# Block sums of the up weights: formed by GpSimd in the front and loaded from DRAM, where they were formed in the up stage

## The chip, the core and the metric

The kernel runs on one core of a Trainium2 chip. A core has TensorE (matmuls, PE in the profile; its weight loads are PEld), VectorE (DVE), ScalarE (ACT), GpSimd (POOL) and SyncE (SP), which here only issues DMAs. All of them work on SBUF, 128 partitions wide; TensorE writes its results to PSUM. Each engine takes its instructions in a fixed order and waits on semaphores. The metric is the time of one execution on the device in microseconds, the median of some runs.

## The reference

One layer of a decoder trunk on 1024 tokens of width 1024, float32. The front mixes three branches and projects them; the second half is a gated feed-forward network, whose input product is the up stage:

```python
h = rms_norm(x, norm1[l]); z = h @ w_in[l]           # pool | q | k | v | u | v | 3 gates
merged = g[:, :, 0] * y_a + g[:, :, 1] * y_b + g[:, :, 2] * y_c
x = x + merged @ w_out[l]
h = rms_norm(x, norm2[l])
up = causal_dwconv(h @ w_up[l], conv_w[l], conv_b[l])   # w_up: 1024 x 5632
gate, val = jnp.split(up, 2, axis=-1)                   # 2816 columns each
x = x + (jax.nn.silu(gate) * val) @ w_down[l]
```

## The kernel before

**Products.** Every float32 factor is split into a high part (ScalarE, a copy rounded to fp32r, L86) and a low part (VectorE, the difference, L87); a product is three matmuls, high-high, high-low and low-high. A weight is loaded into one of three "raw" buffers, split into another buffer, and used.

**The front** goes over the tokens in two halves (t = 0, 1). Each half has the k/v, q and u/v products, then 26 units of 128 columns (`units`: two for pooling, 16 gates of the branches A and C, eight gates of branch B), each of 24 matmuls, after which a gated product of the unit before follows, and at the end the product with w_out. Attention, norms and rope are generators ("tasks") that `tick` advances when a planned clock, counted up with the matmuls that are written, reaches their time. The planned clock sets the order in which the program is written. A scheduler then orders each engine's stream by a timeline of its own, and a transfer whose buffer is free may be issued well ahead of its place in the text. `tc.issue_after(ins)` ties the order of instructions traced in its block to `ins`.

The half's input x is loaded again for the residual into the "x2" buffers (t = 0) or the "x" buffers (t = 1). `part` holds the sum of the branches A and C; it has one buffer. In the second half's w_out product `norm2_flip` normalizes and transposes the first half's result, which stands in x2[0] in SBUF.

**The up stage** uses a Strassen scheme (Winograd's form): for each of 22 chunks of 128 columns the gate block `g` (columns c) and the value block `v` (columns 2816 + c) of w_up are cut into an upper and a lower half of 512 rows, a11, a12 (gate) and a21, a22 (value). Four sums are formed of them by GpSimd (L858 to L861): s1 = a21 + a22, s2 = s1 - a11, s3 = a11 - a21, s4 = a12 - s2. Seven products P1 to P7 follow, each of four times three matmuls, one product being a turn. The first seven chunks do P1 and P2 early (PRE) and the rest later (REST); the other 15 do all in one go (FULL). `up_prep` prepares the weights of a chunk: its loads begin LOADS = 9 turns ahead, its splits are done READY = 7 turns ahead. VectorE adds the products up (L916, L919, L926, L928, L939) and does the convolution (L875) and the gate (L884) of the chunk before. Sums and several of the split weights stand in 13 "q" buffers.

**The down stage** does the same for w_down, from some 1080 us on, and is not touched.

Of the kernel before, what the change touches and what calls it, by code (L numbers as in the profile page):

```python
# [6 lines left out]
F32 = mybir.dt.float32  # L7
# [6 lines left out]
P = 128  # L14
# [19 lines left out]
N_PRE = 7  # L34
PRE_SETS = ((0, 1), (2, 3), (4, 5, 6))
LOADS, READY = 9, 7


def trunk_kernel(tc, x, positions, norm1, w_in, q_norm, k_norm, sinks, w_pool, pool_scale,
# [103 lines left out]
    clock = [0.0]  # L143
    tasks = []

    def tick():
        again = True
        while again:
            again = False
            for tk in list(tasks):  # L150
                if tk[0] <= clock[0] and tk in tasks:
                    step(tk)
                    again = True
# [14 lines left out]
            step(tk)  # L168


    def three(ps, a, b, first, last, n=T):

        pe.matmul(ps, a(0), b(0), start=first, stop=False)  # L173
        pe.matmul(ps, a(0), b(1), start=False, stop=False)  # L174
        r = pe.matmul(ps, a(1), b(0), start=False, stop=last)  # L175
        clock[0] += 3 * n * 0.216 / 512
        return r

# [423 lines left out]
    def up_split(src, wt):  # L602
        split(wt[:, 0], wt[:, 1], src)
        return wt

    def up_early(c):
        g = up_raw(0, c)
        return {n: up_split(a, slot("w", 4, [P, 2, HK, P], F32R)) for n, a in (("P1", g[:, 0:HK, :]), ("P2", g[:, HK:, :]))}
# [29 lines left out]
    x2, sss = [], []  # L638
    h2d = [dp.tile([P, 2, T], F32, name=f"h2d{k}") for k in range(4)]
    gd = [dp.tile([P, S], F32, name=f"gd{c}") for c in range(NC_FF)]  # L640
    mark = [None]
    spawn(setup_rest(), 24)
    st = Stream(w_in, 768, 256, KD, normed.ins)
    for t in range(2):
# [28 lines left out]
        mx = [slot("x", 4, [P, 2, T], F32R) for _ in range(2)]  # L673
        side = [spawn(sgu(u, v, sg))]
        tick()
        part = slot("part", 1, [P, KD, T], F32)
        mxs = [lambda q, m=m: m[:, q, :] for m in mx]
        sgs = [lambda q, m=m: m[:, q, :] for m in sg]
        qv = qa.rearrange("p b (e j q) -> p b e j q", e=2, j=4)
# [29 lines left out]

        wp = None  # L710
        for i, c0 in enumerate(units):
            if i + 1 < len(units):
                wn = w_gran(w_in, units[i + 1])
            else:
                x2t = [slot("x2" if t == 0 else "x", 4, [P, D], F32) for _ in range(NT)]
                for b in range(NT):
                    r = t * T + b * P
                    sp.dma_start(x2t[b], x[r : r + P, :])
                st = Stream(w_out, 0, T, KD)
            if i >= 2:  # L720
                kind, n = ((i - 2) % 2, (i - 2) // 2) if i < 18 else (2, i - 18)
                if kind != 1:
                    wp = proj_b(n) if kind == 2 else proj_ac(n)
            if i == 20 and t == 0:
                load_x(1)
                spawn(h_ahead(1, None))
            if i == 2:
                for q in qt:
                    need(q)
                for b in range(NT):  # L730
                    att.append(spawn(attention(t, b, qa, rqs), 4 + 24 * b))
            ps = mm_ps()
            chan_major(ps, wt, h)
            if i < 2:
                side.append(spawn(pooling(t, i, ps, mx)))
            else:
                th = slot("th", 3, [P, T], F32)
                act.activation(th, ps, AF.Tanh, scale=0.5)
                pend.append((kind, n, th, wp))
                if len(pend) > 1:  # L740
                    finish_unit()
            wt = wn
        while pend:
            finish_unit()
        while tasks:
            step(tasks[0])
        ss = slot("ssx", 2, [P, 32], F32)[:, 0:8]
        if t == 0:
            h = new_h()
            spawn(h_flip(1, h), 0.1)  # L750
        else:
            h2a = new_h()
            spawn(norm2_flip(x2[0], sss[0], h2a, 5, lambda: [a[:, q] for a in [at_ps()] for q in range(2)], 4))
# [82 lines left out]

    def up_prep(c, names):


        ws = wss[c, names]  # L840
        g = up_raw(0, c)
        if names == PRE:
            yield
            for n, a in (("P1", g[:, 0:HK, :]), ("P2", g[:, HK:, :])):
                ws[n] = up_split(a, slot("w", 4, [P, 2, HK, P], F32R))
                yield
            return
        v = up_raw(1, c)
        if names == REST:
            st = held.setdefault(c, {})  # L850
            st["s"], st["ug"] = sm2(), q_([P, S])
            sp.dma_start(st["s"], pre_d[c][:, 0, :])
            sp.dma_start(st["ug"][:, 0:T], pre_d[c][:, 1, :])
        a11, a12, a21, a22 = g[:, 0:HK, :], g[:, HK:, :], v[:, 0:HK, :], v[:, HK:, :]
        sa, sb = q_([P, 2, HK, P]), q_([P, 2, HK, P])
        s1, s2, s3, s4 = sa[:, 0], sa[:, 1], sb[:, 0], sb[:, 1]
        yield
        pool.tensor_tensor(s1, a21, a22, ALU.add)  # L858
        pool.tensor_tensor(s2, s1, a11, ALU.subtract)
        pool.tensor_tensor(s3, a11, a21, ALU.subtract)  # L860
        pool.tensor_tensor(s4, a12, s2, ALU.subtract)  # L861
        for n in names:
            wt = slot("w", 4, [P, 2, HK, P], F32R) if n in ("P1", "P6", "P2") else q_([P, 2, HK, P], F32R)
            ws[n] = up_split({"P1": a11, "P2": a12, "P3": s4, "P4": a22, "P5": s1, "P6": s2, "P7": s3}[n], wt)
            yield

    def conv(u, c):
# [324 lines left out]
```

## Time and profile before

| | |
|---|---|
| median of 3 runs | 1324.67 us (1323.91 to 1326.77) |
| profiled execution | 1327.64 us, its span 1325.9 us |
| TensorE busy | 1285.3 us, 97% of the span |
| VectorE busy | 974.4 us, 73% |
| ScalarE busy | 607.8 us, 46% |
| GpSimd busy | 189.5 us, 14% |
| read from and written to HBM | 120.3 MB and 29.9 MB |
| mean granted clock of TensorE | 0.994 of 2.4 GHz |

The span runs from the first to the last instruction; the execution's own time has some us around it. Busy time is what the profile counts as work of an engine; waiting for a semaphore and issuing a DMA on SP are not in it. Matmuls overlap, so the mean duration of one is longer than the distance from one to the next.

### The profile page before, as it was taken

How to read it: one execution, taken by the hardware profiler on the slowest of the kernel's cores; microseconds unless marked ns; L12 is line 12 of the kernel's file. 1: busy time of each engine (PE TensorE's matmuls, PEld its weight loads, DVE VectorE, ACT ScalarE, POOL GpSimd, SP SyncE). 2: the span in 40 equal slices, each digit the busy share in tenths (PEclk: the TensorE clock that was granted, in tenths of full speed). 3: DMA queues.
4: the chain of work that ended last, by engine and by line, in shares of the span. 5: the costliest groups of instructions: out<-in, count | busy, mean ns of one | idle time of the engine just before them, and what ended most of it. 6: DMA issues, size and time to landing. Idle time of an engine off the chain costs nothing.

```text
span 1325.9 us, 16088 instructions
## 1 busy us (share of the span) xinstructions
PE 1285.3 (97%) x5956; PEld 1064.1 (80%) x5956; DVE 974.4 (73%) x1520; ACT 607.8 (46%) x990; POOL 189.5 (14%) x123
## 2 busy tenths in 40 slices
PE   6999999999999999999999999999999998999996
PEld 6888888888888888888777878878778787788885
DVE  6887875644569776355585889889998885986986
ACT  5655554333465455333573444344444343444441
POOL 0000000000000000000005454245443400101202
PEclk9999999999999999999998999999999999999999
DMA  6422224422432222533554323333232256238705
GB/s 233 118 87 64 80 80 143 115 75 94 148 118 64 81 80 79 152 113 111 200 169 139 104 71 112 112 96 111 81 111 95 80 185 243 48 107 248 122 0 96
DMA packets 167644, 151.25 MB, mean 114 GB/s; under 512 B 7615, under 2 KB 132493, under 8 KB 167565
## 3 DMA queue, kind: packets, MB, share of 16 engines
q1 hardware_dynamic: 163533, 142.87, 33.9%
q0 software_dynamic: 4032, 7.34, 3.7%
q8 instruction: 47, 0.77, 0.2%
q14 instruction: 32, 0.26, 0.1%
HBM read 120.30 MB, written 29.88 MB: 113 GB/s over the span
## 4 chain that ended last, share of the span: by engine, by line
issue 53%; PE 19%; DVE 14%; DMA 5%; ACT 4%; POOL 0%; SPq 0%; POOLq 0%; DVEq 0%; ACTq 0%
DVE x L875 6%; PE bk L1129 4%; PE bk L1128 4%; PE bk L1130 4%; DVE q L87 3%; DMA raw<-in_w_up_dram 3%; PE bk L898 2%; PE bk L899 2%; PE bk L900 2%; ACT x L871 2%; DMA hq<-in_w_down_dram 1%; DVE w L87 1%; ACT w L86 1%; ACT x L883 1%; DVE x L87 1%
## 5 line engine op out<-in xcount | busy, mean ns | idle before, releaser
L175 PE MATMUL mm<-hh,w 128*128 128x512 f32 x416 | 162.6, 391 | 0.0
L173 PE MATMUL mm<-hh,w 128*128 128x512 f32 x416 | 162.6, 391 | 0.0
L174 PE MATMUL mm<-hh,w 128*128 128x512 f32 x416 | 162.4, 390 | 0.0
L87 DVE TENSOR_TENSOR w<-raw,w 128x1024 fp32r<-128x1024 f32 (+1 forms) x96 | 93.3, 976 | 89.5 <-ACT w L86 89.5
L858 POOL TENSOR_TENSOR q<-raw 128x512 f32<-128x512 f32 x22 | 35.6, 1617 | 847.4 <-DVE w L87 653.0
L86 ACT ACTIVATE w<-raw 128x1024 fp32r<-128x1024 f32 (+1 forms) x96 | 82.3, 858 | 155.8 <-PE mm L174 67.1
L875 DVE SCALAR_TENSOR_TENSOR x<-q,cA,x 128x1023 f32<-128x1023 f32 x88 | 136.2, 1554 | 22.8 <-ACT x L871 22.3
L898 PE MATMUL bk<-hq,q 128*128 128x512 f32 x352 | 139.2, 396 | 6.1 <-DVE sm L916 5.9
L899 PE MATMUL bk<-hq,q 128*128 128x512 f32 x352 | 138.0, 392 | 0.0
L900 PE MATMUL bk<-hq,q 128*128 128x512 f32 x352 | 137.6, 391 | 0.0
L1129 PE MATMUL bk<-x,w 128*128 128x512 f32 x308 | 121.1, 393 | 2.5 <-DVE x L87 2.5
L1130 PE MATMUL bk<-w,x 128*128 128x512 f32 x308 | 120.6, 392 | 0.0
L1128 PE MATMUL bk<-w 128*128 128x512 f32 x308 | 93.4, 391 | 4.1 <-ACT w L86 3.8
L174 PEld LDWEIGHTS mm<-hh,w 128*128 128x128 f32 x416 | 78.1, 188 | 16.1
L175 PEld LDWEIGHTS mm<-hh,w 128*128 128x128 f32 x416 | 78.1, 188 | 16.1
L173 PEld LDWEIGHTS mm<-hh,w 128*128 128x128 f32 x416 | 78.1, 188 | 15.7
L87 DVE TENSOR_TENSOR wa<-raw,wa 128x512 fp32r<-128x512 f32 x72 | 49.5, 695 | 55.5 <-ACT wa L86 55.5
L898 PEld LDWEIGHTS bk<-hq,q 128*128 128x128 f32 x352 | 66.6, 189 | 24.4 <-DVE sm L916 8.5
L871 ACT ACTIVATE x<-q,cA 128x1024 f32<-128x1024 f32 x44 | 54.0, 1241 | 68.7 <-DVE q L926 38.0
L86 ACT ACTIVATE wa<-raw 128x512 fp32r<-128x512 f32 x72 | 45.2, 631 | 79.5 <-PE mm L175 67.2
L900 PEld LDWEIGHTS bk<-hq,q 128*128 128x128 f32 x352 | 66.7, 189 | 14.0
L899 PEld LDWEIGHTS bk<-hq,q 128*128 128x128 f32 x352 | 66.7, 189 | 13.7
(267 smaller groups left out, 2957.6 us busy)
## 6 DMA issues: line engine op xcount, KB each, us to landing
raw<-in_w_in_dram SPq DMA_DIRECT2D x72, 512.0 KB, 3.8
raw<-in_w_up_dram SPq DMA_DIRECT2D x51, 512.0 KB, 5.2
gd<-x SPq DMA_DIRECT2D x22, 512.0 KB, 2.8
x<-in_x_dram SPq DMA_DIRECT2D x16, 512.0 KB, 4.0
raw<-in_w_out_dram SPq DMA_DIRECT2D x16, 512.0 KB, 3.7
hq<-gd SPq DMA_DIRECT2D x28, 256.0 KB, 5.3
hq<-in_w_down_dram SPq DMA_DIRECT2D x28, 256.0 KB, 5.6
raw<-in_w_proj_b_dram SPq DMA_DIRECT2D x32, 128.0 KB, 2.7
```

Of the source, the lines that this page charges most:

```text
L86: split.last = act.activation(hi, src, AF.Copy).ins
L87: dve.tensor_tensor(lo, src, f(hi), ALU.subtract)
L173: pe.matmul(ps, a(0), b(0), start=first, stop=False)
L174: pe.matmul(ps, a(0), b(1), start=False, stop=False)
L175: r = pe.matmul(ps, a(1), b(0), start=False, stop=last)
L875: dve.scalar_tensor_tensor(y[:, n:], u[:, 0 : S - n], col(w), y[:, n:], ALU.mult, ALU.add)
L898: pe.matmul(ps, ws[n][:, 0, k, :], rhs[n](0, k), start=start and k == 0, stop=False, skip_group_check=True)
L899: pe.matmul(ps, ws[n][:, 0, k, :], rhs[n](1, k), start=False, stop=False, skip_group_check=True)
L900: pe.matmul(ps, ws[n][:, 1, k, :], rhs[n](0, k), start=False, stop=k == HK - 1, skip_group_check=True)
L1128: pe.matmul(ps[i], hi[:, 0, ts], hi[:, 1, :], start=start, stop=False, skip_group_check=True)
L1129: pe.matmul(ps[i], hi[:, 0, ts], lo[:, 1, :], start=False, stop=False, skip_group_check=True)
L1130: pe.matmul(ps[i], lo[:, 0, ts], hi[:, 1, :], start=False, stop=q == b - 1, skip_group_check=True)
```

## The change

The 22 chunks' sums are formed in the front. A second kind of generator (`side_line`, one at a time) is advanced by `tick`. `weight_sums` loads the two blocks of a chunk, forms the four sums in place on GpSimd, with the operations that the up stage had, and stores s3 and s1 (in v's buffer) and s2 and s4 (in g's buffer) to a DRAM tile `s_d[c]` from GpSimd's queue. The chunks come in three sets: six, written from unit 16 of the first half on, in the "x2" buffers (two for each chunk, four in all); eight, written from the end of the first half's units on, in the one "part" buffer, which holds two chunks; and eight, written from unit 13 of the second half on, in the "x2" buffers again. What is left of a set is written at once by `side_end`, at the last unit or at unit 2. Since the third set takes x2[0]'s buffers, the first half's result is loaded again from `out` before norm2_flip.

In the up stage `up_prep` then loads the four sums of a chunk as two transfers of 512 KB in place of the GpSimd additions, the gate block only for PRE and FULL, and only the lower half of the value block.

```diff
--- before.py
+++ after.py
@@ -34,6 +34,8 @@
 N_PRE = 7
 PRE_SETS = ((0, 1), (2, 3), (4, 5, 6))
 LOADS, READY = 9, 7
+SUM_SETS = (range(0, 6), range(6, 14), range(14, 22))
+SUM_GAPS = (8.2, 8.6, 8.2)
 
 
 def trunk_kernel(tc, x, positions, norm1, w_in, q_norm, k_norm, sinks, w_pool, pool_scale,
@@ -143,7 +145,18 @@
     clock = [0.0]
     tasks = []
 
+    side_line = []
+
+    def side_step():
+
+        try:
+            side_line[0][0] = clock[0] + next(side_line[0][1])
+        except StopIteration:
+            side_line.pop(0)
+
     def tick():
+        while side_line and side_line[0][0] <= clock[0]:
+            side_step()
         again = True
         while again:
             again = False
@@ -168,11 +181,13 @@
             step(tk)
 
 
+    last_pe = [None]
+
     def three(ps, a, b, first, last, n=T):
 
         pe.matmul(ps, a(0), b(0), start=first, stop=False)
         pe.matmul(ps, a(0), b(1), start=False, stop=False)
-        r = pe.matmul(ps, a(1), b(0), start=False, stop=last)
+        r = last_pe[0] = pe.matmul(ps, a(1), b(0), start=False, stop=last)
         clock[0] += 3 * n * 0.216 / 512
         return r
 
@@ -603,6 +618,54 @@
         split(wt[:, 0], wt[:, 1], src)
         return wt
 
+    def weight_sums(cs, tiles, gap):
+
+
+        def take(c):
+            vg = tiles()
+            for o, dst in zip((1, 0), vg):
+                c0 = o * D_FF + c * P
+                with tc.issue_after(last_pe[0].ins):
+                    sp.dma_start(dst, w_up[:, c0 : c0 + P].rearrange("(k p) c -> p k c", p=P))
+            return vg
+
+        nxt = take(cs[0])
+        yield gap
+        for j, c in enumerate(cs):
+            v, g = nxt
+            a11, a12, a21, a22 = g[:, 0:HK], g[:, HK:], v[:, 0:HK], v[:, HK:]
+            with tc.issue_after(last_pe[0].ins):
+                pool.tensor_tensor(a22, a21, a22, ALU.add)
+            pool.tensor_tensor(a21, a11, a21, ALU.subtract)
+            pool.dma_start(s_d[c][:, 1], v)
+            pool.tensor_tensor(a11, a22, a11, ALU.subtract)
+            pool.tensor_tensor(a12, a12, a11, ALU.subtract)
+            pool.dma_start(s_d[c][:, 0], g)
+            yield gap / 2
+            if j + 1 < len(cs):
+                nxt = take(cs[j + 1])
+                yield gap / 2
+
+    def own_tiles():
+        return [slot("x2", 4, [P, KD, P], F32) for _ in range(2)]
+
+    def part_tiles():
+        big = slot("part", 1, [P, 4, KD, P], F32)
+        turn = [0]
+
+        def tiles():
+            turn[0] ^= 2
+            return big[:, turn[0]], big[:, turn[0] + 1]
+
+        return tiles
+
+    def side_work(cs, tiles, gap):
+        side_line.append([clock[0], weight_sums(cs, tiles, gap)])
+
+    def side_end():
+        while side_line:
+            side_step()
+
     def up_early(c):
         g = up_raw(0, c)
         return {n: up_split(a, slot("w", 4, [P, 2, HK, P], F32R)) for n, a in (("P1", g[:, 0:HK, :]), ("P2", g[:, HK:, :]))}
@@ -638,6 +701,7 @@
     x2, sss = [], []
     h2d = [dp.tile([P, 2, T], F32, name=f"h2d{k}") for k in range(4)]
     gd = [dp.tile([P, S], F32, name=f"gd{c}") for c in range(NC_FF)]
+    s_d = [dp.tile([P, 2, KD, P], F32, name=f"ws{c}") for c in range(NC_FF)]
     mark = [None]
     spawn(setup_rest(), 24)
     st = Stream(w_in, 768, 256, KD, normed.ins)
@@ -673,7 +737,6 @@
         mx = [slot("x", 4, [P, 2, T], F32R) for _ in range(2)]
         side = [spawn(sgu(u, v, sg))]
         tick()
-        part = slot("part", 1, [P, KD, T], F32)
         mxs = [lambda q, m=m: m[:, q, :] for m in mx]
         sgs = [lambda q, m=m: m[:, q, :] for m in sg]
         qv = qa.rearrange("p b (e j q) -> p b e j q", e=2, j=4)
@@ -709,9 +772,15 @@
 
         wp = None
         for i, c0 in enumerate(units):
+            if i == (16 if t == 0 else 13):
+                side_work(SUM_SETS[2 * t], own_tiles, SUM_GAPS[2 * t])
+            if i == 2:
+                side_end()
+                part = slot("part", 1, [P, KD, T], F32)
             if i + 1 < len(units):
                 wn = w_gran(w_in, units[i + 1])
             else:
+                side_end()
                 x2t = [slot("x2" if t == 0 else "x", 4, [P, D], F32) for _ in range(NT)]
                 for b in range(NT):
                     r = t * T + b * P
@@ -746,6 +815,12 @@
             step(tasks[0])
         ss = slot("ssx", 2, [P, 32], F32)[:, 0:8]
         if t == 0:
+            side_work(SUM_SETS[1], part_tiles(), SUM_GAPS[1])
+        else:
+            for b in range(NT):
+                x2[0][b] = slot("x2", 4, [P, D], F32)
+                sp.dma_start(x2[0][b], out[b * P : (b + 1) * P, :])
+        if t == 0:
             h = new_h()
             spawn(h_flip(1, h), 0.1)
         else:
@@ -836,32 +911,33 @@
 
     def up_prep(c, names):
 
-
         ws = wss[c, names]
-        g = up_raw(0, c)
+        if names != REST:
+            g = up_raw(0, c)
         if names == PRE:
             yield
             for n, a in (("P1", g[:, 0:HK, :]), ("P2", g[:, HK:, :])):
                 ws[n] = up_split(a, slot("w", 4, [P, 2, HK, P], F32R))
                 yield
             return
-        v = up_raw(1, c)
+        v = raw([P, HK, P])
+        c0 = D_FF + c * P
+        sp.dma_start(v, w_up[T:, c0 : c0 + P].rearrange("(k p) c -> p k c", p=P))
         if names == REST:
             st = held.setdefault(c, {})
             st["s"], st["ug"] = sm2(), q_([P, S])
             sp.dma_start(st["s"], pre_d[c][:, 0, :])
             sp.dma_start(st["ug"][:, 0:T], pre_d[c][:, 1, :])
-        a11, a12, a21, a22 = g[:, 0:HK, :], g[:, HK:, :], v[:, 0:HK, :], v[:, HK:, :]
+        yield
         sa, sb = q_([P, 2, HK, P]), q_([P, 2, HK, P])
-        s1, s2, s3, s4 = sa[:, 0], sa[:, 1], sb[:, 0], sb[:, 1]
-        yield
-        pool.tensor_tensor(s1, a21, a22, ALU.add)
-        pool.tensor_tensor(s2, s1, a11, ALU.subtract)
-        pool.tensor_tensor(s3, a11, a21, ALU.subtract)
-        pool.tensor_tensor(s4, a12, s2, ALU.subtract)
+        sp.dma_start(sa, s_d[c][:, 0].rearrange("p (j k) c -> p j k c", j=2))
+        sp.dma_start(sb, s_d[c][:, 1].rearrange("p (j k) c -> p j k c", j=2))
+        ab = {"P3": sa[:, 1], "P4": v, "P5": sb[:, 1], "P6": sa[:, 0], "P7": sb[:, 0]}
+        if names == FULL:
+            ab["P1"], ab["P2"] = g[:, 0:HK, :], g[:, HK:, :]
         for n in names:
             wt = slot("w", 4, [P, 2, HK, P], F32R) if n in ("P1", "P6", "P2") else q_([P, 2, HK, P], F32R)
-            ws[n] = up_split({"P1": a11, "P2": a12, "P3": s4, "P4": a22, "P5": s1, "P6": s2, "P7": s3}[n], wt)
+            ws[n] = up_split(ab[n], wt)
             yield
 
     def conv(u, c):
```

## Rows read from the trace of the kernel before

**Rows 1.** Page, part 1: engine, busy us, share of the span, instructions.
```profile
PE 1285.3 (97%) x5956; PEld 1064.1 (80%) x5956; DVE 974.4 (73%) x1520; ACT 607.8 (46%) x990; POOL 189.5 (14%) x123
```

**Rows 2.** Table by stretch: length, busy us of each engine, granted clock, DMA share, GB/s.
```profile
54.00:78.00 24.00, 24.00 (x130) 20.15 (x129) 22.17 (x49) 15.60 (x28) 0.00 (x0) 1.00 0.32 94
...
288.00:343.00 55.00, 55.00 (x290) 46.99 (x289) 24.92 (x38) 22.11 (x43) 0.00 (x0) 1.00 0.35 115
343.00:433.00 90.00, 89.42 (x459) 75.51 (x459) 68.49 (x160) 50.16 (x91) 0.00 (x0) 1.00 0.31 91
490.00:606.00 116.00, 116.00 (x533) 96.56 (x533) 63.32 (x105) 46.93 (x81) 0.00 (x0) 1.00 0.41 121
700.00:1075.00 375.00, 365.71 (x1587) 298.44 (x1586) 327.66 (x339) 159.45 (x228) 162.65 (x88) 0.99 0.31 97
705.00:712.00 7.00, 5.86 (x14) 4.66 (x15) 4.25 (x6) 2.61 (x6) 1.72 (x2) 0.51 0.55 165
```

**Rows 3.** TensorE's waits: us in total, times, longest.
```profile
PE bk L898 <- DVE sm L916: 5.9, 6, 1.8
...
PE at L174 <- DVE t L87: 0.6, 1, 0.6
```

**Rows 4.** Timeline, 705 to 707 us: start, us, instruction, idle time before it.
```profile
706.14 0.80 PE L898 MATMUL bk<-hq,w 128*128 128x512 f32 x1 [3.20 <-ACT w L86]
```

**Rows 5.** VectorE's groups by shape, 700 to 1075 us: busy us, mean ns, idle before.
```profile
L875 DVE SCALAR_TENSOR_TENSOR x<-q,cA,x 128x1022 f32<-128x1022 f32 x40 | 67.4, 1685 | 0.4
L87 DVE TENSOR_TENSOR q<-q,q 128x512 fp32r<-128x512 f32 x64 | 65.5, 1032 | 8.4 <-ACT q L86 8.3
L875 DVE SCALAR_TENSOR_TENSOR x<-q,cA,x 128x1023 f32<-128x1023 f32 x40 | 59.1, 1477 | 17.8 <-ACT x L871 17.6
L87 DVE TENSOR_TENSOR q<-raw,q 128x512 fp32r<-128x512 f32 x21 | 27.3, 1298 | 0.0
...
L916 DVE TENSOR_TENSOR sm<-sm,bk 128x512 f32<-128x512 f32 x21 | 14.2, 677 | 0.0
```

**Rows 6.** Chain of work, 745 to 756 us: one L875 while GpSimd is idle.
```profile
747.82 1.28 DVE x L875
```

**Rows 7.** Timeline: TensorE's transposes, and the splits of VectorE they read.
```profile
76.13 0.69 DVE L87 TENSOR_TENSOR t<-t,t 128x512 fp32r<-128x512 f32 x1
...
77.18 0.81 PE L428 MATMUL at<-identr,t 128*128 128x128 f32 x8
...
391.26 0.69 DVE L87 TENSOR_TENSOR t<-t,t 128x512 fp32r<-128x512 f32 x1
...
393.38 0.81 PE L428 MATMUL at<-identr,t 128*128 128x128 f32 x8
```

**Rows 8.** Timeline of GpSimd: one addition while VectorE is idle.
```profile
702.11 1.27 POOL L860 TENSOR_TENSOR q<-raw,raw 128x512 f32<-128x512 f32 x1
```

**Rows 9.** Timeline of the start: DMA issues on SP, and the last L208 of VectorE.
```profile
5.26 2.92 SPq L233 DMA_DIRECT2D raw<-in_w_in_dram  x3
...
12.46 3.97 SPq L718 DMA_DIRECT2D x<-in_x_dram  x4
...
13.76 0.75 DVE L208 TENSOR_SCALAR x<-x,rs 128x1024 f32<-128x1024 f32 x1
```

**Rows 10.** Timeline: the first matmul of the output projection, the stores of the first half.
```profile
288.01 0.39 PE L173 MATMUL mm<-wa,t 128*128 128x512 f32 x1
...
334.73 2.25 SPq L762 DMA_DIRECT2D out_dram<-x  x3
```

**Rows 11.** DMA issues: count, KB each, median us to landing.
```profile
out_dram<-x SPq DMA_DIRECT2D x8, 512.0 KB, 7.3
...
out_dram<-sm POOLq DMA_DIRECT2D x16, 256.0 KB, 5.2
```

**Rows 12.** Line L1045, GpSimd's issue of a DMA: ns min/median/max.
```profile
L1045 POOL DMA_DIRECT2D out_dram<-sm x16: 865/887/1559, 1139.9 to 1317.9; - x16
```

## The prediction

> **What bounds the kernel now.** I read the busy times first: TensorE works in 1285.3 of 1325.9 us, VectorE in 974.4 [rows 1]. So only what lets TensorE wait, or what slows its clock, can move the time. The table by stretch comes next. In the front (to some 650 us) TensorE has no gap worth naming; in the up stage, 700 to 1075 us, it is busy 365.7 of 375, VectorE 327.7 and GpSimd 162.7 in 88 instructions, and from 705 to 712 us the granted clock is 0.51, the lower of its two levels (1.2 GHz) [rows 2]. The waits of TensorE say who was late: six times the addition at L916 (5.9 us together), and the weight split L86, for which TensorE waits 3.2 us until 706.1 [rows 3, 4]. The reader is to see that the up stage is where VectorE is nearly full.
>
> **What the change removes.** The four GpSimd additions of each of 22 chunks leave the up stage. They hurt there because they slow VectorE: L875 means 1685 and 1477 ns where it takes 1280 alone, the 128x512 splits 1032 and 1298 where they take 690 [rows 5, 6, 7]. Excess: 40 x 0.405 + 40 x 0.197 + 64 x 0.34 + 21 x 0.61 = 16.2 + 7.9 + 21.8 + 12.8 = 58.7 us, or 2.7 us for each chunk. GpSimd pays too: 162.65 / 88 = 1.85 us for an addition that takes 1.27 alone [rows 2, 8]. L916, which reads PSUM and one SBUF operand, stays at 677 ns throughout [rows 5]. The Trainium skill (SBUF — State Buffer, "Who interferes with whom") gives a reason: a pair of ports is locked for a whole instruction, and a VectorE operation with two SBUF inputs competes for it with a GpSimd read. If each addition held VectorE up for its whole 1.27 us, a chunk would cost 5.1 us, ten chunks from 343 us on 51 instead of 27, and the forecast below would be some 24 us higher; the trace shows half of that, and the sum goes by the trace.
>
> So after the change VectorE's 327.7 us of the up stage become about 269, and the six waits (5.9 us) go. The wait of 3.2 us until 706 also ends on a chain through the sums (load, GpSimd, L86); with the sums ready in DRAM it goes, and the slow clock behind it: 7 us at 0.51, at half speed, which costs 3.4 us [rows 2, 4]. Sum: 5.9 + 3.2 + 3.4 = 12.5 us. Bounds 4 (only part of the six) and 13; I take 11.5.
>
> **What it adds in the up stage.** 44 loads of 512 KB, less seven gate loads and half of 22 value loads: 22 - 3.5 - 5.5 = 13 MB more. At 97 GB/s the DMA share is 0.31 [rows 2], so a full share moves some 313 GB/s, and 13 MB are 42 us in 375: 0.31 becomes 0.42. The loads need a "q" buffer, not a result, and 13 of those rotate; I cost them at nothing, under cover of the seven turns by which weights are prepared ahead. Without it the 3.2 us before 706 come back with its clock: 6.6 us.
>
> **Where the sums go to.** The diff's text puts them at three stretches: from unit 16 of the first half, the output projection, and unit 13 of the second half, with issue_after on the last matmul. That call orders only what is traced on the engine of the named instruction. The kernel has the case already: the first w_in loads are traced behind the last L208 of VectorE, which runs at 13.76 us, and SP issued them at 5.26. And the loads of L718, written in the last unit of the first half (some 277 us), were issued at 12.46 [rows 9]: what has a free buffer goes out at once. Here SP and POOL work is queued behind a TensorE instruction, so I expect the buffers alone to place it:
> - Set 0 (6 chunks) has the four "x2" buffers, free from the start: about 12 to 68 us. L718 is pushed behind it; its data is first read near 310, so that costs nothing.
> - Set 1 (8 chunks) needs "part", free when the last gated unit is done, at 288.0 us. Set 2 (8 chunks) needs "x2" again, free when the stores at 334.7 land (median 7.3 us): about 343 [rows 10, 11]. The reload of x2[0] then has 150 us in hand and costs nothing; were set 2 late, norm2_flip would wait for it.
>
> The pace of a chunk: alone 4 x 1.27 + 2 x 0.88 (the issue of a DMA on GpSimd) = 6.8 us, beside VectorE 4 x 1.85 + 1.8 = 9.2 [rows 2, 8, 12]. With two buffers and a store that takes over 5 us to land [rows 11], about 9. So some 6 chunks from 288 to 343 and the other 10 from 343 to 433.
>
> **What that costs.** VectorE's idle time in each stretch [rows 2] against 2.7 us for each chunk:
> - 288 to 343: 30.1 us idle, 16 asked: hidden. At unit 16 and later it would be hidden as well, and after 490 too (52.7 idle in 116 us).
> - 54 to 78: 1.8 us idle; the last two chunks of set 0 ask 5.4: 3.6 too much. TensorE follows at once: the transposes at 77.18 read a split of 0.69 us begun at 76.13, 0.36 us before [rows 7]. Cost 3.6 (0 to 5).
> - 343 to 433: 21.5 us idle, ten chunks ask 27: at least 5.5 too much. It isn't spread evenly: the transposes at 393.38 follow a split that ends at 391.95 [rows 7], and at 412 TensorE waits 0.6 us for VectorE even now [rows 3]. With some 5 us late at 393 and 3.5 more at 412: 8.5 (5.5 to 16).
> - The clock: the 3.2 us wait before 706 was followed by 3.4 us lost at the lower level. For three waits of 3 to 5 us I take 4 together (0 to 10).
> - The queues: a chunk's load waits on SP for its buffer, and the w_in loads of the front stand behind it. If SP's order was laid out for 6.8 us and a chunk takes 9.2, ten chunks fall behind by 24 us; how far the loads run ahead the trace doesn't show. And 2 MB in 9 us is 233 GB/s, 0.74 of a full share beside the 0.31 of this stretch. 0 to 24; I take 2, since the weights have three raw buffers.
>
> Sum: 3.6 + 8.5 + 4 + 2 = 18.1 lost, 11.5 won: 6.6 us slower than the profiled execution, 1327.64 to 1334.2. That execution stands 2.97 us over the median of 1324.67, so I say 1331.
>
> **Rivals.**
> - *The front hides it* (chance 0.36). The delays of VectorE fall where TensorE has other matmuls queued, or the text's stretches hold. For it: in the up stage VectorE lost 58.7 us and TensorE only 5.9. Against it: the two tight places above. Then 8 to 12 us are kept, 0 to 4 lost: 1313 to 1321. It decides in my favour once the front gives more than 11.5 us away.
> - *SP is blocked* (0.12, part of the slower side). Loads of w_in stand behind chunk loads whose buffers come late. For it: 0.74 + 0.31 is over a full share. Against it: after its start TensorE waits for no load in the front now. 15 of the 24 us reach TensorE: 1324.67 + 3.6 + 8.5 + 4 + 15 - 11.5 = 1344. The Trainium skill (SBUF — State Buffer, "A bandwidth-pool intuition that's wrong") has a rule that would lengthen this: GpSimd can't write DMA descriptors while VectorE runs a two-port copy. The trace has stores from the POOL queue that land in 5.2 us; none ran beside such work.
> - *Gains and losses cancel* (0.17): the front loses 9 to 14 us, 1322 to 1327.
> - *The up stage isn't freed* (0.05, slower side): sums loaded late take the place of sums formed late; 6.6 us are not won, 1338.
>
> **How the numbers follow.** My forecast, the front paying 14 us or more through VectorE, has 0.30; with SP blocked and the up stage not freed the slower side has 0.47. Its own range is 1327.5 to 1348. For 8 in 10 the range reaches over the hidden front: 1313 to 1348, with some 0.08 below and 0.1 above. Changes under 0.2% (2.65 us) can't be told from none here: faster 0.36, the same 0.17, slower 0.47.
>
> **What would show it.** GpSimd's additions between 15 and 70 us and from 288 to about 433, none at 490 to 600: my placement. If they stand at 207 to 285 and 490 to 600 instead, the text's places hold and the hidden front is right. New waits of TensorE for VectorE near 77, 393 and 412, with a lower granted clock after them; L875 at about 1280 ns and no wait for L916 after 700; SP waiting for POOL's stores with w_in loads late would be the second rival. The forecast is wrong if TensorE stays gapless from 343 to 433 in spite of additions there.

## The result, and the profile after

The changed kernel is slower: 1366.54 us median of 6 runs (1360.62 to 1369.46) against 1325.24 of 6 runs before, ratio 1.0302 (1.0281 to 1.0322), 41 us. The profiled execution of the changed kernel took 1360.62 us with a span of 1358.8; it is the fastest of its six, so its profile shows 33 us of loss where the median has 41.

The first view is the busy time of each engine and, from the 40 slices of 34 us, GpSimd, the clock and the DMA share. Lines of the changed kernel:

```profile
PE 1295.3 (95%) x5956; PEld 1071.0 (79%) x5956; DVE 984.1 (72%) x1520; ACT 611.1 (45%) x990; POOL 177.0 (13%) x167
...
POOL 4430000006575510000000000000000000101202
PEclk9999999999978999999999999999999999999998
DMA  8862222528999752254356454344344347228705
```

TensorE does as many matmuls as before [rows 1], GpSimd's work has moved to slices 1 to 3 and 10 to 15, and in those slices the DMA share is 5 to 9 tenths. The table by stretch says what that cost (columns: length, busy time of TensorE, its weight loads, VectorE, ScalarE, GpSimd, granted clock, DMA share, GB/s). The last line is the up stage, which begins some 46 us later here:

```profile
12.00:54.00 42.00, 35.44 (x200) 30.55 (x201) 39.22 (x68) 16.82 (x30) 24.20 (x23) 0.99 0.90 275
54.00:78.00 24.00, 24.00 (x114) 19.76 (x114) 23.65 (x28) 13.06 (x22) 14.72 (x12) 0.94 0.76 230
78.00:125.00 47.00, 41.41 (x206) 33.95 (x205) 40.38 (x101) 25.28 (x45) 3.56 (x4) 0.96 0.47 149
310.00:361.00 51.00, 50.02 (x266) 42.64 (x265) 29.38 (x33) 20.71 (x41) 33.42 (x32) 1.00 0.88 279
361.00:479.00 118.00, 98.97 (x461) 79.47 (x460) 100.83 (x155) 49.83 (x90) 73.84 (x63) 0.91 0.90 278
479.00:700.00 221.00, 221.00 (x1042) 184.51 (x1041) 134.86 (x261) 98.50 (x184) 2.00 (x3) 1.00 0.39 119
750.00:1125.00 375.00, 375.00 (x1657) 310.74 (x1656) 278.90 (x346) 167.72 (x230) 0.00 (x0) 1.00 0.44 141
```

The up stage is won: TensorE has no gap in 375 us, where it was busy 365.7, and VectorE needs 279 where it needed 327.7 [rows 2]. The front is lost: TensorE idles 6.6 us from 12 to 54, 5.6 from 78 to 125 and 19.0 from 361 to 479. Four stretches of it run at the lower clock level (0.50, 1.2 GHz):

```profile
53.30:56.50 3.20, 2.97 (x7) 2.42 (x8) 3.20 (x4) 1.58 (x2) 3.07 (x2) 0.50 0.40 127
84.00:87.30 3.30, 3.30 (x10) 2.56 (x9) 3.30 (x7) 0.00 (x0) 0.00 (x0) 0.50 0.92 267
377.60:391.00 13.40, 7.18 (x16) 5.16 (x17) 11.34 (x9) 1.78 (x3) 10.68 (x10) 0.50 1.11 339
428.80:435.40 6.60, 5.55 (x13) 4.40 (x14) 6.29 (x21) 5.12 (x12) 0.97 (x2) 0.50 0.65 199
```

TensorE had stood still for 2.7, 3.7, 4.1 and 5.0 us just before or at the start of them; the third holds a second wait, of 4.2 us. It is busy for 19.0 us in the four, half of which, 9.5, is what the clock cost. TensorE's waits name the late one (columns: us in total, times, longest); the six waits for the old L916 and the wait for L86 in the up stage [rows 3, 4] are gone, and in their place stand waits of the front, for the splits of the weight tiles "wa" (L89 and L88 are the old L87 and L86):

```profile
PE mm L189 <- DVE wa L89: 14.0, 6, 4.2
...
PE mm L188 <- ACT t L733: 5.0, 1, 5.0
PE mm L188 <- ACT wa L88: 4.1, 1, 4.1
...
PE at L189 <- DVE t L89: 2.8, 2, 1.7
PE at L484 <- DVE st L467: 2.4, 1, 2.4
```

One such place, in the timeline of the changed kernel (start, us, instruction, idle time before it in brackets):

```profile
378.96 1.15 ACT L88 ACTIVATE wa<-raw 128x512 fp32r<-128x512 f32 x2 [8.87 <-DMA raw<-in_w_in_dram]
379.28 1.27 POOL L638 TENSOR_TENSOR x<-x 128x512 f32<-128x512 f32 x1
...
379.62 6.22 DVE L89 TENSOR_TENSOR wa<-raw,wa 128x512 fp32r<-128x512 f32 x1 [7.22 <-ACT wa L88]
...
380.51 1.26 POOL L642 TENSOR_TENSOR part<-part 128x512 f32<-128x512 f32 x1
...
381.74 1.25 POOL L639 TENSOR_TENSOR x<-x,x 128x512 f32<-128x512 f32 x1
382.94 0.57 POOL L643 DMA_DIRECT2D ws<-part  x1
383.54 1.27 POOL L638 TENSOR_TENSOR x<-x 128x512 f32<-128x512 f32 x1
384.75 0.57 POOL L640 DMA_DIRECT2D ws<-x  x1
385.34 1.64 POOL L641 TENSOR_TENSOR x<-x,x 128x512 f32<-128x512 f32 x1
...
385.90 0.80 PE L189 MATMUL mm<-wa,hh 128*128 128x512 f32 x1 [4.18 <-DVE wa L89]
```

The raw weights come late (ScalarE waited 8.87 us for the load); then a split that takes 0.69 us alone [rows 7] lasts 6.22, through the rest of one addition and three whole ones, of two sets at once. Each of these takes 1.25 to 1.27 us, no more than alone [rows 8]. TensorE resumes when the split ends.

How late TensorE runs is worked out by matching the k-th matmul of one trace with the k-th of the profile before (5956 in both). Columns: the instant in the profile before. Rows: us later (+) or earlier than there.

```
at                 25    55   125   343   360   395   450   600   690   710  1075
changed           -0.1   7.9  16.4  17.8  29.1  41.7  45.2  45.3  46.5  41.7  31.4
gain alone        -0.0   0.1   0.0   0.0   0.1   0.2  -0.1  -0.0  -1.0  -6.8 -17.0
no additions      -0.5   3.2   7.2   7.1   7.4  11.0   9.9  10.0   8.9   3.2  -7.1
eighth of bytes   -0.4  13.8  19.4  22.7  35.5  48.8  56.0  56.0  55.2  49.4  39.1
held               1.2   1.3   1.3   2.1   2.5   8.4   8.1   8.2  10.9   5.1  -5.2
set 0 free        -0.2  12.2  20.8  22.1  24.1  28.4  28.1  28.2  32.4  26.4  16.2
breaks, ordered    1.4   4.6  15.3  15.3  25.0  38.9  44.3  44.5  43.4  37.8  27.5
one operand        1.9   5.0  13.0  13.0  13.1  23.2  21.8  22.0  20.9  15.4   5.1
write only         1.6   1.7   2.5   2.5   4.6   8.8   6.6   6.7   6.9   1.6  -8.7
held, paced 2     -0.3  -0.2  -0.3  -0.3   0.1   0.2  -0.1  -0.0   2.0  -3.8 -14.1
```

The first line says where the time went: 16.4 us before 125, 1.4 from there to 343, 27.4 from 343 to 450; after 690 some 15 come back. Of the 45 us, 30.4 are TensorE's idle time (32.2 in the table above, less 1.8 that it had before) and 9.5 the lower clock; the other 5 these rows do not resolve. The other lines belong to the experiments.

### The profile page after: what moved, and what is told of

It is laid out like the page before. It is cut to its first block, busy times and chain, and to the rows that moved or that the text cites. A ratio compares the mean times of both kernels' runs of the same rounds, so it can differ in the third digit from the quotient of the medians.

```text
span 1358.8 us, 16338 instructions
## 1 busy us (share of the span) xinstructions
PE 1295.3 (95%) x5956; PEld 1071.0 (79%) x5956; DVE 984.1 (72%) x1520; ACT 611.1 (45%) x990; POOL 177.0 (13%) x167
## 5 line engine op out<-in xcount | busy, mean ns | idle before, releaser
L89 DVE TENSOR_TENSOR w<-raw,w 128x1024 fp32r<-128x1024 f32 (+1 forms) x96 | 97.1, 1013 | 71.2 <-ACT w L88 71.2
L88 ACT ACTIVATE w<-raw 128x1024 fp32r<-128x1024 f32 (+1 forms) x96 | 82.3, 857 | 123.0 <-PE mm L189 56.6
L951 DVE SCALAR_TENSOR_TENSOR x<-q,cA,x 128x1023 f32<-128x1023 f32 x88 | 112.0, 1279 | 19.3 <-ACT x L947 18.8
L89 DVE TENSOR_TENSOR wa<-raw,wa 128x512 fp32r<-128x512 f32 x72 | 75.9, 1067 | 50.8 <-ACT wa L88 50.8
L1121 POOL DMA_DIRECT2D out_dram<-sm x16 | 14.4, 978 | 715.5 <-ACT sm L1133 704.4
L189 PE MATMUL mm<-wa,hh 128*128 128x512 f32 (+1 forms) x192 | 72.0, 377 | 14.0 <-DVE wa L89 14.0
L88 ACT ACTIVATE wa<-raw 128x512 fp32r<-128x512 f32 x72 | 44.7, 629 | 86.9 <-PE mm L190 54.8
L974 PEld LDWEIGHTS bk<-hq,q 128*128 128x128 f32 x352 | 66.1, 188 | 13.7
L975 PEld LDWEIGHTS bk<-hq,q 128*128 128x128 f32 x352 | 66.1, 188 | 13.7
```

The source lines that it names most:

```text
L88: split.last = act.activation(hi, src, AF.Copy).ins
L89: dve.tensor_tensor(lo, src, f(hi), ALU.subtract)
L951: dve.scalar_tensor_tensor(y[:, n:], u[:, 0 : S - n], col(w), y[:, n:], ALU.mult, ALU.add)
L974: pe.matmul(ps, ws[n][:, 0, k, :], rhs[n](0, k), start=start and k == 0, stop=False, skip_group_check=True)
L975: pe.matmul(ps, ws[n][:, 0, k, :], rhs[n](1, k), start=False, stop=False, skip_group_check=True)
```

## The experiments

**The gain by itself.** Only chunk 0's sums are formed, and every chunk of the up stage loads those; the other chunks' sums are left out.

```diff
-SUM_SETS = (range(0, 6), range(6, 14), range(14, 22))
+SUM_SETS = (range(0, 1), range(0, 0), range(0, 0))
-        sp.dma_start(sa, s_d[c][:, 0]...)    # the same for sb
+        sp.dma_start(sa, s_d[0][:, 0]...)
```

> Only chunk 0's sums are formed and stored; the up stage loads these two transfers for every chunk, so the other 21 chunks' sums are left out. It shows what the up stage gives back by itself. By the prediction's first part (12.5 us of waits and slow clock go, 11.5 kept) 1314 us, 1311 to 1318. If loading the sums cost the up stage something of its own, 1320 or more.

1313.25 us, ratio 0.9909 (0.9893 to 0.9925): 12 us are won in the up stage, with all 44 loads in it. So against this kernel the front costs 1.0302 - 0.9909, 52 us.

**The transfers by themselves.** Loads and stores of all 22 chunks stay where they were; the additions are left out, so what is stored are no sums.

```diff
-            with tc.issue_after(last_pe[0].ins):
-                pool.tensor_tensor(a22, a21, a22, ALU.add)
-            pool.tensor_tensor(a21, a11, a21, ALU.subtract)
...
-            pool.tensor_tensor(a11, a22, a11, ALU.subtract)
-            pool.tensor_tensor(a12, a12, a11, ALU.subtract)
```

> The four GpSimd additions of each chunk are left out; the same blocks are loaded and stored as they are, at the same places in the text. Theory A (the front's loss of some 53 us comes from transfers: full DMA engines and the weight loads of the front queued on SP behind the chunk loads): 1345 to 1365, as the transfers stay. Theory B (the loss comes from the additions, which hold VectorE up at the shared port, single splits by 4 to 6 us): 1311 to 1322.

1322.12 us, ratio 0.9972 (0.9959 to 0.9985), at the upper end of theory B's range. The transfers cost 0.9972 - 0.9909, 8 us; the additions the other 44.

**The additions by themselves.** All additions stay. Of each set the first two chunks are loaded whole and the first is stored whole; of the others an eighth is loaded and stored. The up stage loads the sums of each set's first chunk, and those of the other chunks are left out.

```diff
+                if n < 2:
                     sp.dma_start(dst, w_up[:, c0 : c0 + P]...)
+                else:
+                    sp.dma_start(dst[:, 3:4], w_up[0:P, c0 : c0 + P]...)
...
```

> All 88 additions stay; each set loads and stores two pairs of blocks whole and then only an eighth of the rows of each further chunk, and the up stage loads the sums of each set's first chunk (so the sums of the others are left out). Theory A: the DMA engines are free again, 1311 to 1322. Theory B: the additions follow each other even more closely, 1340 to 1365. Both in part: between, and the part of each can be read against the run without additions.

1368.91 us, ratio 1.0331 (1.0306 to 1.0357), no better than the whole change, and a little over theory B's range. Without loads to wait for, GpSimd's additions stand closer, and VectorE does less. From 26 to 40 us, table by stretch of this run:

```profile
26.00:40.00 14.00, 10.48 (x52) 8.65 (x52) 13.93 (x13) 3.65 (x8) 10.95 (x11) 0.88 0.41 137
```

VectorE is busy throughout, and gets through 13 instructions. SP and its queue, which is what this run relieves, are not what most of the loss comes from.

**The sets held at the text's stretches.** The chunk loads are ordered on SP behind SP's own latest load of front weights, which does hold them. The output is complete.

```diff
-        sp.dma_start(rw, w[:, c0 : c0 + P]...)
+        last_raw[0] = sp.dma_start(rw, w[:, c0 : c0 + P]...)
...
-                with tc.issue_after(last_pe[0].ins):
+                with tc.issue_after(last_raw[0].ins):
                     sp.dma_start(dst, w_up[:, c0 : c0 + P]...)
```

> The chunk loads are tied on SP behind the last weight load of the front that stands ahead of them in the text, so that the sets run at the stretches that the text names. Theory C (it is the bunching of the sets, 12 to 82 and 310 to 482 us, that costs; spread out, both additions and transfers are covered): 1311 to 1320, faster than before. If additions or transfers cost as much wherever they stand: 1340 to 1365.

1323.51 us, ratio 0.9983 (0.997 to 0.9996), between the two ranges: 42 us of the 52 are gone by nothing but other places. The additions run at 195 to 279, 298 to 383 and 503 to 610 us:

```profile
195.00:290.00 95.00, 94.50 (x421) 77.96 (x420) 57.81 (x102) 35.49 (x61) 41.25 (x36) 1.00 0.86 252
290.00:343.00 53.00, 53.00 (x273) 44.97 (x273) 32.50 (x39) 22.22 (x43) 31.41 (x30) 1.00 0.92 290
343.00:433.00 90.00, 84.60 (x434) 70.38 (x434) 74.06 (x143) 44.00 (x73) 19.86 (x19) 1.00 0.58 186
...
490.00:606.00 116.00, 116.00 (x533) 96.60 (x532) 72.82 (x104) 45.28 (x81) 49.48 (x45) 1.00 0.84 239
```

Most of the loss left is in the third line, where VectorE is fullest: 5.4 us with 19 additions and DMA issues of GpSimd, against half a microsecond with 111 in the other three. (Another 2.9 us go from 606 to 640; 2.2 go there in the held run without additions too, so they are not the additions'.) By line and shape, with the same operation free of overlap as the measure, VectorE is delayed by some 40 us here and by some 60 us in the changed kernel (56 to 65 by how the undisturbed time is taken). The additions cost the whole time some 9 us here, by the held run without them below, and 44 there.

**Breaks between the additions, first try.** After each addition two short memsets of a tile that nothing reads.

```diff
             pool.tensor_tensor(a21, a11, a21, ALU.subtract)
+            [pool.memset(rest, 0.0) for _ in range(2)]
...    # the same behind the other three
```

> After each of the four additions GpSimd runs two short write-only memsets (256 columns, of a tile that nothing reads), so that no two additions stand back to back; all else is the changed kernel, and the output is complete. Theory (a VectorE operation with two SBUF operands that loses once stays held until the row of back-to-back additions ends): single splits that took 4 to 6 us in the changed kernel take at most 2.5 us, TensorE's waits of 3 to 5 us at the weight splits go, and the ratio falls from 1.030 to between 1.00 and 1.018 (1325 to 1349 us). Rival (it is the total time of the additions beside VectorE that counts, however they are spaced): each addition costs the same, GpSimd only gets longer, 1360 to 1375 us, ratio 1.027 or more.

1368.88 us, ratio 1.0325 (1.0307 to 1.0344). All 176 memsets ran before 125 us, since nothing ordered them; the run decides nothing about the rest.

**Held, without additions.** The chunk loads held as above, and the additions left out.

> The chunk loads tied on SP behind the last weight load, as in the run that held the sets at the stretches of the text, and the additions left out: chunks are loaded and stored unsummed, so the output lacks the sums. Theory (of the 10 us that the held order still lost against the gain alone, most are the additions that slow VectorE; the transfers cost only where ten chunks are bunched): 1312 to 1317 us, ratio 0.990 to 0.994. Rival (the transfers cost their 9 us wherever they stand): 1319 to 1323 us, ratio 0.995 to 0.998.

1314.11 us, ratio 0.9914 (0.9901 to 0.9927), in the theory's range. Held, the transfers cost nothing that can be measured (0.9914 against 0.9909); what the held order still loses, 0.9983 - 0.9914 or 9 us, is its additions.

**Held and paced.**

```diff
-SUM_SETS = (range(0, 6), range(6, 14), range(14, 22))
-SUM_GAPS = (8.2, 8.6, 8.2)
+SUM_SETS = (range(0, 8), range(8, 13), range(13, 22))
+SUM_GAPS = ((2.4, 7.7), (4.3, 4.3), (2.4, 7.7))
...
-            if i == (16 if t == 0 else 13):
+            if i == (14 if t == 0 else 13):
```

> The held order with the sets cut anew (8, 5 and 9 chunks; the first from unit 14 of the first half) and the two halves of a chunk's pause made unequal, so that the next chunk's load is asked for sooner after the additions. Complete output. Theory (what the held order still lost are few places where the additions of a chunk meet a split that TensorE waits for, above all in the middle set, where VectorE is fullest): with three chunks fewer there, 1314 to 1320 us, ratio 0.991 to 0.996. Rival (every chunk costs TensorE about the same wherever it is put): 1322 to 1325 us, ratio 0.997 to 1.000.

1325.0 us, ratio 0.9994 (0.9986 to 1.0003): the theory's range was missed. The middle set no longer cost anything, but the pauses of the outer sets came out longer than written (at first 14 to 21 us from chunk to chunk where 10.1 was written), so the last chunks of these sets came in a heap at their ends: TensorE waited 3.2 us, from 286 to 289, for the weights of a branch's projection ("wp") and 3.2 us in four waits from 610 to 620.

**Held and paced, with breaks.** The same with the unordered memsets.

> The run before with the two memsets behind each addition. Complete output. Theory (rows of back-to-back additions hold VectorE): at least 2 us under the run without the breaks, 1312 to 1317 us. Rival (only the total time on GpSimd counts): the same as without breaks or up to 4 us more.

1326.98 us, 1.0011 (1.0000 to 1.0021). All memsets ran before 75 us here, so it says nothing of breaks.

**Breaks in their order.** The changed kernel, each memset ordered behind its addition and the next addition of the chunk behind the memset.

```diff
...
+        r = pool.tensor_tensor(*a)
+        for _ in range(2):
+            with tc.issue_after(r.ins):
+                r = pool.memset(rest, 0.0)
+        return tc.issue_after(r.ins)
...
```

> As the run with the breaks, but each memset is ordered behind its addition and the next addition of the chunk behind the memset; in the earlier run the memsets had no order and ran in a block before 120 us, so it said nothing of 300 to 485. Complete output. Theory (a VectorE operation waits for a row of back-to-back additions): the single splits of 4 to 6 us shrink to at most 2.5 us and the ratio falls to 1.000 to 1.018 (1325 to 1349 us). Rival (the total of the additions counts, however they are spaced): 1360 to 1375 us, ratio 1.027 or more, since GpSimd's whole work per chunk only grows.

1358.35 us, ratio 1.0243 (1.0219 to 1.0266), between the two ranges. The long holds did go: no VectorE instruction lasts over 2.5 us in the front, and the splits of "wa" from 300 to 500 us take 991 ns each where they took 1319 from 300 to 485 in the changed kernel:

```profile
L89 DVE TENSOR_TENSOR wa<-raw,wa 128x512 fp32r<-128x512 f32 x33 | 32.5, 991 | 38.0 <-ACT wa L88 38.0
```

The time gave back only 8 us. So the theory fell for the most part: one split caught in a row of additions is the most striking picture in the trace, but not where most of the 44 us went. VectorE is still delayed by some 40 to 60 us in all, by how it is counted, and TensorE still runs 44 us late at 450.

**Only the first set free.** The held kernel, with the first set's loads as in the changed one.

```diff
...
+                with tc.issue_after((last_pe if c in SUM_SETS[0] else last_raw)[0].ins):
...
```

> Only the loads of the first set (6 chunks) go out when their buffers are free, at the start of the run; the other two sets stay held at the stretches of the text. Complete output. Theory (the loss of 53 us in the front is the sum of what the two bunched stretches lose, and by the gaps and the clock of the changed kernel's profile some 14 us of it lie before 125 us): held order plus 12 to 18 us, 1335 to 1342 us, ratio 1.008 to 1.013. Rival (nearly all of the loss comes from the stretch where two sets run at once, 370 to 475 us): 1323 to 1329 us, ratio 0.998 to 1.003.

1344.27 us, ratio 1.014 (1.0118 to 1.0161). Set 0 at the start costs 1.014 - 0.9983, 21 us, above both ranges. Sets 1 and 2 free instead of held cost the rest, 1.0302 - 1.014, another 21. With the 10 us that remain when all are held the 52 us are accounted for.

**Held and paced, second try.**

```diff
+SUM_SETS = (range(0, 7), range(7, 13), range(13, 22))
+SUM_GAPS = ((3.0, 4.8), (4.3, 4.3), (3.0, 4.8))
...
+            if i == (14 if t == 0 else 12):
```

> The held order with 7, 6 and 9 chunks, the first set from unit 14 of the first half, the last from unit 12 of the second, and shorter pauses, so that the last two chunks of a set no longer come in a heap behind the last unit (the held and paced run lost 3.2 us at 285 and some 4 us from 610 to 619 there). Complete output. Theory (what is left of the loss is that heap): 1316 to 1321 us, ratio 0.993 to 0.997. Rival (each chunk costs TensorE about half a microsecond wherever it is): 1323 to 1327 us, ratio 0.998 to 1.001.

1320.53 us, ratio 0.9959 (0.9943 to 0.9975), as the theory had it: the fastest complete kernel of the study, some 5 us under the kernel before. Its seven runs go from 1313.06 to 1321.61, and the profiled one is the fastest. In it TensorE is on time until 600 us with all the additions in the front. The median run is 7 us longer than the gain by itself, and no trace shows where it loses them. The profiled run:

```profile
195.00:290.00 95.00, 95.00 (x425) 78.68 (x424) 60.11 (x105) 36.39 (x63) 37.82 (x34) 1.00 0.85 255
290.00:343.00 53.00, 53.00 (x281) 45.38 (x280) 31.19 (x37) 21.89 (x43) 33.24 (x31) 1.00 0.93 295
...
490.00:606.00 116.00, 116.00 (x533) 96.60 (x532) 70.55 (x103) 45.49 (x79) 55.29 (x48) 1.00 0.92 264
606.00:640.00 34.00, 31.72 (x147) 25.70 (x146) 21.54 (x44) 15.90 (x30) 0.00 (x0) 1.00 0.47 166
```

In the first stretch VectorE takes some 9 us more than without the additions (60.11; 50.97 in the same stretch of the gain by itself), and TensorE does not wait.

**What in an addition it is.** Two runs with the changed kernel's placement, loads and stores, and no sums: four GpSimd multiplications of one 128x512 operand by 1 in place of the additions, and ten memsets of 128x512.

```diff
...
-            pool.tensor_tensor(a21, a11, a21, ALU.subtract)
+            pool.tensor_scalar(a21, a21, 1.0, None, ALU.mult)
...    # the other three likewise
```

> The changed kernel's placement, loads and stores, but the four GpSimd additions of a chunk are four multiplications by 1 of one 128x512 operand each, so the sums are missing from the output. Theory (what delays VectorE is GpSimd's reading of two operands at a time, the same thing that a VectorE operation with two SBUF operands wants): little delay, 1318 to 1330 us, ratio 0.995 to 1.003, as without additions. Rival (any GpSimd operation that reads SBUF holds VectorE for its length): the loss per us of GpSimd's time stays as it was, 1345 to 1370 us, ratio 1.015 or more.

1328.19 us, ratio 1.0013 (1.0002 to 1.0025). The profiled run, 1334.58, is the slowest of its eleven, so its line in the table of lateness shows more than the median lost. Two groups of GpSimd, and one of VectorE from 300 to 485 us (busy us, mean ns):

```profile
L642 POOL TENSOR_SCALAR x<-x 128x512 f32<-128x512 f32 x14 | 24.3, 1738 | 0.0
L641 POOL TENSOR_SCALAR x<-x 128x512 f32<-128x512 f32 x14 | 23.2, 1656 | 13.4 <-DMA x<-in_w_up_dram 13.2
...
L89 DVE TENSOR_TENSOR wa<-raw,wa 128x512 fp32r<-128x512 f32 x33 | 23.9, 728 | 33.4 <-ACT wa L88 33.4
```

GpSimd is busy for longer than with the additions (1.64 us an operation in the mean of all 88, where an addition took 1.45), and the splits take 728 ns instead of 1319.

> The same placement, loads and stores, with ten GpSimd memsets of 128x512 in place of the four additions of a chunk (ten by 0.52 us is about the 5.1 us of the additions); the sums are missing from the output. Theory (only reading GpSimd operations hold VectorE): as without additions, 1318 to 1328 us, ratio 0.995 to 1.002, VectorE's splits at 0.69 us. Rival (GpSimd's time as such, with its later stores and loads, is what TensorE pays): 1340 us or more, ratio 1.011 or more.

1325.7 us, ratio 0.9991 (0.9976 to 1.0006), and the splits are as they are alone:

```profile
L89 DVE TENSOR_TENSOR wa<-raw,wa 128x512 fp32r<-128x512 f32 x31 | 21.0, 698 | 39.0 <-ACT wa L88 39.0
```

Both runs lie in the range of their first theory. Over the run without additions, writing costs 0.0019 or 2.5 us, which is not clear of noise, reading one operand 0.0041 or 5.4, reading two 0.0330 or 44. So it is the two-operand addition that costs, not GpSimd's time nor the later stores. The multiplication is another instruction as well as one operand less; the two were not tried apart.

## Why the prediction was right in sign and wrong in size

The forecast was 6.6 us slower, 1331 us; measured were 41 us more, 1366.54, over the range's end of 1348.

- **The gain** was forecast at 11.5 us and measured at 12. L951, the old L875, takes 1279 ns in the up stage, its time alone [rows 5, 6]; the waits for the sums are gone; the loads are hidden, at a DMA share of 0.44 where 0.42 was worked out. How close the number came is in part luck: in the two profiles 5.8 us are won from 690 to 710, where 6.6 was forecast, and 10.2 from there to 1075, where the six waits are 5.9; the waits do not show the other 4.
- **The placement** was right: GpSimd's additions run from 19 to 81 us (set 0), 310 to 404 (set 1) and 379 to 480 (set 2), placed by free buffers and not by the text, and none in the second half's projection. Each set is later than forecast (12 to 68, from 288, from 343), the last two in a kernel that by then runs 16 to 29 us late. Without that step the forecast would have been the hidden front.
- **The price for VectorE**, 2.7 us a chunk, was right: some 60 us over 22 chunks is 2.7. The Trainium skill (SBUF — State Buffer, "Who interferes with whom") has GpSimd and VectorE shut each other out for a whole instruction; by full holds the price was 5.1. Single splits were held longer than one addition (6.22 us), which goes further than the page. On average the trace shows about half of a full hold, as in the up stage before.
- **The step that failed is "VectorE's idle time in each stretch against 2.7 us for each chunk".** It took an idle microsecond of VectorE for a free one. From 12 to 54 us the prediction charged nothing: by its rule four chunks ask 11 us there, and VectorE is idle for 12.5, as the table by stretch of the kernel before has it:

```profile
12.00:54.00 42.00, 40.81 (x234) 35.85 (x235) 29.46 (x75) 22.25 (x39) 1.18 (x1) 1.00 0.53 168
```

  Yet TensorE is 7.9 us late by 55; the whole first set was priced at 3.6 us and measured at 21. From 343 on 8.5 was forecast, together with the clock's 4 and the queues' 2 14.5, and 27 was measured in the trace, clock and queues included. The waits also came elsewhere: of the three places that the prediction named, the transposes near 77 and 393 did not wait and the one at 412 cost 1.7 us (at 456), while most of the long waits for VectorE are for splits of "wa", near 48, 54, 84 and 386.

  Idle time says nothing of how soon a result is needed. VectorE's idle time before "wa" is a wait for ScalarE's half of the same split (38.0 us of 38.0 in the row of the ordered breaks), so it comes before the work. What a delay meets first is the time that the low part lies ready before the first matmul that reads it, its lead. In the kernel before, the k-th split matched with the k-th weight tile's first such matmul gives (us; the first column says when the splits start):

```
                                        least  median  most
14 to 69, k/v, q and u/v, first half      1.8     3.7   7.7
267 to 328, projection                    2.0     4.8  23.2
331 to 388, k/v, q and u/v, second half   2.0     4.1   5.6
146 to 268, gated units                   6.1     8.0  10.9
465 to 587, gated units                   4.9     7.6  10.9
```

  One pair of a gated unit and one of the second half's first products, from the timeline of the kernel before:

```profile
221.08 1.23 DVE L87 TENSOR_TENSOR w<-raw,w 128x1024 fp32r<-128x1024 f32 x1 [3.72 <-ACT w L86]
...
228.62 0.39 PE L175 MATMUL mm<-hh,w 128*128 128x512 f32 x1
...
372.72 0.69 DVE L87 TENSOR_TENSOR wa<-raw,wa 128x512 fp32r<-128x512 f32 x1
...
376.42 0.39 PE L174 MATMUL mm<-wa,hh 128*128 128x512 f32 x1
```

  A hold of 4 to 6 us, or some late work of VectorE and a late load, uses up a lead of 4 us: in the changed kernel 7 of the 20 splits of the first group and 9 of those of the third end less than 1 us before their matmul, and none does before. In the gated units of the held kernels the same additions delay VectorE by 9 to 13 us in each half, the lead stays at 3.2 us or more, and TensorE loses half a microsecond at most. So the additions cost TensorE 44 us for VectorE's 60 in the one placement and 9 for 40 in the other; in the up stage before, TensorE waited 5.9 us for VectorE's 58.7. How full VectorE is does not say it alone: from 361 to 479 it was 85% busy, additions included, and TensorE stood still for 19 us of 118; in the up stage before it was 87% busy, for 9 of 375. Nor does the lead alone: in the first half's projection it was hardly longer than in the stages beside it, single splits were held for up to 5.8 us, and TensorE lost 1.4 us from 125 to 343, with VectorE 58% busy from 310 to 361. No run changed the lead, or VectorE's other work, by itself, so what share each has stays open.
- **The clock** was sized at 4 us (0 to 10), for three waits of 3 to 5 us; with five waits of 2.7 to 5.0 us it cost 9.5, inside the bounds and over the value taken.
- **The queues** were sized at 2 us (0 to 24); the transfers cost 8 in the free placement and nothing in the held one.
- **The rivals.** "The front hides it" was wrong for this kernel; of the held kernels the second paced one, 1320.53, is in its range of 1313 to 1321, and the others lie over it. "SP is blocked" is not what most of it was: with an eighth of the bytes the time stays at 1368.9, and the transfers alone cost 8 us. "Gains and losses cancel" is the first held run. "The up stage isn't freed" is excluded by the first experiment.

The sum with what was measured: 12 won; 21 lost by set 0 at the start, 21 by sets 1 and 2 running at once, and 10 that the first held order loses too: 40, as the ratio says.

## What to carry to other kernels

When work on one engine slows another, do not set the delay against that engine's idle time: look at how long each of its results lies ready before it is read, and at what else that engine has to do there. Here a stage in which TensorE did not wait had a lead of only 2 to 5 us. Prefer stretches in which TensorE has its operands ready well ahead, and check by a trace that the order written is the order on the queue. Before moving an operation, ask whether it reads two operands from SBUF: here four such additions a chunk cost 44 us over 22 chunks where one-operand work of greater length cost 5.

## What the runs showed of the hardware that was not expected

- A VectorE operation with two SBUF operands can be held through several GpSimd additions in a row, and through the DMA issues between them: 6.22 us for a split of 0.69, with GpSimd at its undisturbed 1.25 to 1.27 us per addition. With breaks no operation lasted over 2.5 us.
- Beside GpSimd's one-operand multiplications (1.64 us each in the mean, 1.48 the shortest) VectorE's splits took 728 ns, beside its memsets (0.53 us each) 698, beside its additions 1319.
- In the up stage both sides paid: an addition took 1.85 us instead of 1.27 [rows 2, 8], and VectorE lost 2.7 us a chunk. In the front of the changed kernel VectorE lost as much, and an addition took 1.45 us in the mean.
- Waits of TensorE of 2.7 to 5 us went with 3.2 to 6.6 us at the lower clock level each, two of 4 us close together with 13.4; this cost 9.5 of the 45 us. Waits of 2.2 and 2.4 us, at 48 and 474, went with none.
